# Moving the tiles that TensorE reads to other address offsets within 512 bytes

## The chip, the cores and the metric

The kernel runs on one core of a Trainium2 chip. The metric is device time in microseconds of the whole program on that core, the median of several executions. The profiled execution is one of its own, and every duration below is from it.

## The reference

One layer of a hybrid decoder on a sequence of 512 positions of width 2048, in float32:

```
h = rms_norm(x, norm1_w);  proj = h @ w_in            # 2048 -> 5648 columns
q, k, v, z, xbc, dt = split(proj)
attn = moba_attention(rms_norm(q), rms_norm(k), v)    # 8 heads x 128, blocks of 256
ssm  = grouped_rms_norm(ssd_scan(silu(conv4(xbc)), softplus(dt)) * silu(z))
x = x + concat(attn, ssm) @ w_out                     # 2048 -> 2048
h = rms_norm(x, norm2_w)
u = conv3(h @ w_up)                                   # 2048 -> 2 x 5632
x = x + (silu(u_gate) * u_val) @ w_down               # 5632 -> 2048
```

## The kernel before

Every float32 product is made of three matmuls on numbers that are cut in two: with hi the rounded part (type float32r) and lo the rest, it adds hi·hi, hi·lo and lo·hi. ScalarE makes hi (a Copy), VectorE makes lo (a subtraction).

**First stage** (to about 800 us): the input projection, attention, the scan, and the output projection. The activations lie in 16 tiles `A0` to `A15` (hi) and 16 tiles `B0` to `B15` (lo), each 128 x 512 float32, in the pool `ab`. Weights come by DMA into `raw` (three buffers), pieces of up to 528 columns are cut into `hi` and `lo` (three buffers each, pool `w`). All matmuls of this stage have the source line 183, a helper that paces them. There are two forms. In `acc<-A,hi`, `acc<-B,hi`, `acc<-A,lo` the activations are the moving operand (512 columns) and a 128 x 128 block of weights is loaded as the stationary one. In `acc<-hi,A`, `acc<-lo,A`, `acc<-hi,B` it is the other way round, and 256, 264 or 512 columns of weights move. In the names of the profile the moving operand of these stands first.

**Second stage** (from about 800 us): up-projection and down-projection, with a Strassen-like scheme of seven products in place of eight. A group is one block of rows of output (44 groups for the up-projection, 24 for the down-projection); a group has seven items, and an item is one product: eight blocks of 128 x 128 weights (seven in 16 of the down-projection's groups), each with three matmuls of 256 columns. Line 1286 is hi·hi, line 1287 hi·lo (the same weights loaded again), line 1289 lo·hi; an item is 8 x (1286, 1287) and then 8 x 1289, 24 matmuls in a row. The weights of an item lie in `hi2` (three buffers of 4096 bytes, made by ScalarE at line 1041) and `lo2` (two buffers, VectorE, line 1050). The moving operand is one of seven combinations of the activations, the kinds KT1, KT3, K11, KT2, K21, K22, KT4, held in the tiles `cmb0` to `cmb6` in this order. A kind is a tile of 16384 bytes a partition, [hi or lo][8 blocks][256 columns], so each matmul's moving operand starts at the tile's address plus a multiple of 1024 bytes, and each block of weights at its tile's address plus a multiple of 512. `cmb0` to `cmb4` lie in the pool `cmb` on the right side of the memory, `cmb5` and `cmb6` in the pool `w2` on the left side, behind the weights. The items of a group come in the order P5, P3, P1, P4, P6, P2, P7, which are the kinds KT1, K22, K11, KT4, KT2, K21, KT3 (P3 and P4 belong to the group before). P2 alone writes a tile `y`; the others write a tile `x`.

What a tile's address is, is decided by the pools: a pool lays its tiles one behind the other, in the order in which they are first asked for. The order of all instructions is written out in the program (slots, and a planner for the first stage that uses estimated costs); no address has a part in it.

Of the kernel before, what the change touches and what calls it, by code (L numbers as in the profile page):

```python
# [20 lines left out]
F32 = mybir.dt.float32  # L21
F32R = mybir.dt.float32r
# [37 lines left out]

KT1, KT3, K11, KT2, K21, K22, KT4 = range(7)
PLACE = [4, 5, 0, 6, 2, 3, 7]
KIND = {"P5": KT1, "P7": KT3, "P1": K11, "P6": KT2, "P2": K21, "P3": K22, "P4": KT4}


# [122 lines left out]
def body(ctx, tc, xT, wi, wz, wo, wu, wd0, wd1, wd2, pp, pf, outT, dbg={}):  # L188
    nc = tc.nc
    clk = {"pe": 0.0, "act": 0.0, "dve": 0.0, "pool": 0.0, "last": ("pe", 0.0)}  # L190
    V, A_, T, G = (Paced(e, k, clk) for e, k in
                   ((nc.vector, "dve"), (nc.scalar, "act"), (nc.tensor, "pe"), (nc.gpsimd, "pool")))

    consts = ctx.enter_context(tc.tile_pool(name="consts", bufs=1))
    pstack = ExitStack()
    psum = pstack.enter_context(tc.tile_pool(name="psum", bufs=4, space=bass.MemoryType.PSUM))
    dram = ctx.enter_context(tc.tile_pool(name="scratch", bufs=1, space=bass.MemoryType.DRAM))
    ab, cw, work = ExitStack(), ExitStack(), ExitStack()
    wpool = ab.enter_context(tc.tile_pool(name="w", bufs=3))
    abp = ab.enter_context(tc.tile_pool(name="ab", bufs=1))  # L200
    cpool = cw.enter_context(tc.tile_pool(name="c", bufs=1, side="right"))
    wk = work.enter_context(tc.tile_pool(name="work", bufs=1, side="right"))
# [7 lines left out]


    RW = 1024
    BEHIND = 2.5
    pieces = []

# [14 lines left out]
    def issue_dma(upto):  # L230
        while state["dma"] <= min(upto, len(raw_q) - 1):
            ci = state["dma"]
            src, width = raw_q[ci]
            r = wpool.tile([128, RW], F32, name="raw")
            if ci == 0:
                nc.sync.dma_start(r[:, :512], src[:, :512])
                nc.sync.dma_start(r[:, 512:width], src[:, 512:])
            else:
                nc.sync.dma_start(r[:, :width], src)
            raws[ci] = r  # L240
            state["dma"] += 1

    def issue_split(upto):
        while state["split"] <= min(upto, len(pieces) - 1):
            i = state["split"]
            ci, o, w, _ = pieces[i]
            issue_dma(ci)
            h = wpool.tile([128, 528], F32R, name="hi")
            l = wpool.tile([128, 528], F32R, name="lo")
            src = raws[ci][:, o:o + w]  # L250
            clk["last"] = ("pe", clk["pe"])
            A_.activation(h[:, :w], src, AF.Copy)
            V.tensor_tensor(l[:, :w], src, h[:, :w].bitcast(F32), op=OP.subtract)
            his[i] = (h, l)
            ready[i] = clk["dve"]
            state["split"] += 1

    def dump(n, ap):
        if n in dbg:
            nc.sync.dma_start(dbg[n], ap)  # L260


    A = [abp.tile([128, S], F32R, name=f"A{k}") for k in range(NK)]
    B = [abp.tile([128, S], F32R, name=f"B{k}") for k in range(NK)]
    C = [cpool.tile([128, S], F32, name=f"C{k}") for k in range(NK)]
    par = consts.tile([128, NPC], F32, name="par")
# [12 lines left out]
    def pc(name, i=0, n=1):  # L279
        o = _PC[name] + i  # L280
        return (p2["par"] if name[0] == "f" else par)[:, o:o + n]
# [54 lines left out]
    def step(e):  # L336
        clk["last"] = ("pe", clk["pe"])
        old = clk["pe"], clk["act"], clk["dve"], clk["pool"]
        e[3] = 0
        try:  # L340
            say = next(e[0])
        except StopIteration:
            if e in gens:
                gens.remove(e)
            return
        if old != (clk["pe"], clk["act"], clk["dve"], clk["pool"]):
            e[1] = max(clk[k] for k in ("pe", "act", "dve", "pool") if k != "pool" or clk[k] != old[3]) + 0.3
        if e not in gens:
            e[2] = e[2] or say == "soon"
            gens.append(e)  # L350
        elif say == "soon":
            e[2] = True
        elif say == "later":
            e[2] = False

    def advance(force=False):

        for e in list(gens):
            e[3] += 1
            ready_ = clk["pe"] >= e[1]  # L360
            if force or (e[2] and (ready_ or e[3] > 1)) or \
                    (ready_ and max(clk["act"], clk["dve"]) < clk["pe"] + BEHIND):
                step(e)
# [308 lines left out]
    def tok_use(k0, nk, cols, box, done):  # L672

        def use(h, l):
# [5 lines left out]
            for kk, t in order:  # L680
# [3 lines left out]
                o = box["acc"][t][:, :cols]  # L684
                T.matmul(o, A[k][:, ts_], h[:, cc], start=k == 0, stop=False)
                T.matmul(o, A[k][:, ts_], l[:, cc], start=False, stop=False)
                T.matmul(o, B[k][:, ts_], h[:, cc], start=False, stop=k == NK - 1)
                if k == NK - 1:
                    done(t, box["acc"][t])
        return use  # L690

    XR = lambda k: (A[k], B[k])

# [8 lines left out]
    def prep_x(k):  # L702
        t = ssq_box[k]
        A_.activation(A[k], t, AF.Copy, scale=pc("nw1", k))
        V.scalar_tensor_tensor(B[k], t, pc("nw1", k), A[k].bitcast(F32), op0=OP.mult, op1=OP.subtract)

# [131 lines left out]
    def split_mix(i):  # L838
# [5 lines left out]
        dump("mix%d" % k, C[k])  # L844
        A_.activation(A[i], C[k], AF.Copy)
        V.tensor_tensor(B[i], C[k], A[i].bitcast(F32), op=OP.subtract)

    p2 = {}

    def phase2():  # L850
        while gens:
            advance(True)
        work.close()
        cw.close()
        p2["cmb"] = ctx.enter_context(tc.tile_pool(name="cmb", bufs=1, side="right"))
        p2["kinds"] = [None] * 7
        for t in (KT1, KT3, K11, KT2, K21):
            p2["kinds"][t] = cmb_tile(t)
        p2["pool"] = work.enter_context(tc.tile_pool(name="work2", bufs=1, side="right"))
        p2["ssq"] = rbc  # L860

    def cmb_tile(t):

        pool = p2["cmb"] if t < K22 else p2["cmbl"]
        return pool.tile([128, 2, 8, 256], F32R, name="cmb%d" % t)
# [26 lines left out]
    def g_x2(acc, i):  # L892

        if "pool" not in p2:
            phase2()
            for n in range(4):
                load_xin(n)
# [17 lines left out]
        for n, ts in enumerate(((KT1, K11), (KT2, K21, KT3))):  # L915
            sums(V, g, n)
            for t in ts:
                o = p2["kinds"][t][:, :, i // 2, :]
                A_.activation(o[:, 0], g[:, PLACE[t], :], AF.Copy)
                V.tensor_tensor(o[:, 1], g[:, PLACE[t], :], o[:, 0].bitcast(F32), op=OP.subtract)  # L920
        nc.sync.dma_start(xd[:, i // 2], g[:, 3:8:4, :])
        square(t_, i)

    last_acc = []
    MR = lambda k: (A[k], B[k])
    out_start = len(pieces)
# [17 lines left out]
    V.memset(u_t[:, 0:3], 0.0)  # L944
    prep_x(0)
    issue_split(0)
    sq_x(0)
    issue_split(1)
    prep_x(1)
    sq_x(1)  # L950
    prep_x(2)
    issue_split(2)
    sq_x(2)
    mix_at = {}
# [15 lines left out]
    lp = ctx.enter_context(tc.tile_pool(name="w2", bufs=1, reuse_waits="tile"))  # L970
# [3 lines left out]
    def side_tile(pool, shape, name, bufs=1):  # L974
        return pool.tile([128] + shape, F32, name=name, bufs=bufs)
# [68 lines left out]
    def split_lo(k):  # L1044
        if k >= len(items):
            return
        n = cols(items[k][0])
        h, src = parts[k]
        l = lp.tile([128, 1024], F32R, name="lo2", bufs=2)
        ve.tensor_tensor(l[:, :n], src[:, :n], h[:, :n].bitcast(F32), op=OP.subtract)  # L1050
        parts[k] = (h, l)
# [24 lines left out]
    def b_load(k):  # L1076
# [6 lines left out]
        else:  # L1083
            ld = side_tile(box["pool"], [4, 256], "ld", box["depth"])
        sy.dma_start(ld[:, :m, :], gd[p][:, 4 * h:4 * h + m, PLACE[t], :])
        lds.append(ld)
# [34 lines left out]
    def x_load(n):  # L1121
        if n < 4:
            x_ld.append(side_tile(box["pool"], [4, 256], "ld", 3))
            sy.dma_start(x_ld[n], xd[:, 4 * (n % 2):4 * (n % 2) + 4, n // 2, :])

    def x_split(n):
        t, h = (K22, KT4)[n // 2], n % 2
        if h == 0:
            up_kinds[t] = cmb_tile(t)
        o = up_kinds[t][:, :, 4 * h:4 * h + 4, :]  # L1130
        se.activation(o[:, 0], x_ld[n], AF.Copy)
        ve.tensor_tensor(o[:, 1], x_ld[n], o[:, 0].bitcast(F32), op=OP.subtract)
        x_load(n + 3)

    for n, slot in enumerate((2, 4, 5, 6)):
        at(slot, x_split, n)
# [117 lines left out]
    def step_slot(slot):  # L1254
        run(slot)
        if slot > -2:
            split_lo(slot + 2)
        run(slot, after)
        split(slot + 3)

    for slot in range(min(events), -3):
        run(slot)
    step_slot(-3)
    split_lo(0)
    spawn(g_x2(last_acc[0], NK - 1))
    while gens:
# [5 lines left out]
    for k, (gi, x) in enumerate(items):  # L1272
# [6 lines left out]
        h, l = parts.pop(k)  # L1279
        bk = g["kinds"][KIND[x]]  # L1280
        n = g["n"]
# [36 lines left out]
```

## Time and profile before

| | us |
|---|---|
| median of 3 runs | 2114.42 (2113.61 to 2114.91) |
| the profiled execution's own time | 2114.84 |
| its span from the first to the last instruction | 2113.1 |
| TensorE matmul busy | 2073.9 (98%) |
| TensorE weight load busy | 1949.7 (92%) |
| VectorE busy | 1583.5 (75%) |
| ScalarE busy | 988.3 (47%) |

A matmul's busy time runs from its start to its end, and the next one begins long before that end. The rate of TensorE is therefore read from the distance between two starts, or from the number of matmuls in a stretch, not from the mean time of one.

### The profile page before, as it was taken

How to read it: one execution, taken by the hardware profiler on the slowest of the kernel's cores; microseconds unless marked ns; L12 is line 12 of the kernel's file. 1: busy time of each engine (PE TensorE's matmuls, PEld its weight loads, DVE VectorE, ACT ScalarE, POOL GpSimd, SP SyncE). 2: the span in 40 equal slices, each digit the busy share in tenths (PEclk: the TensorE clock that was granted, in tenths of full speed). 3: DMA queues.
4: the chain of work that ended last, by engine and by line, in shares of the span. 5: the costliest groups of instructions: out<-in, count | busy, mean ns of one | idle time of the engine just before them, and what ended most of it. 6: DMA issues, size and time to landing. Idle time of an engine off the chain costs nothing.

```text
span 2113.1 us, 37694 instructions
## 1 busy us (share of the span) xinstructions
PE 2073.9 (98%) x15366; PEld 1949.7 (92%) x15366; DVE 1583.5 (75%) x2251; ACT 988.3 (47%) x1433; POOL 207.9 (10%) x107
## 2 busy tenths in 40 slices
PE   9999999999999998999999999999999899999999
PEld 7888887888888878999999999999999899899999
DVE  6545555345555558999999999999999977977976
ACT  5433435244344435555555555555555534534532
POOL 0020000000000001111110111011111111101110
PEclk9999999999999999999999999999999999999999
DMA  5233222332225535445444444454455667856763
GB/s 194 75 115 91 71 75 76 99 101 80 80 70 172 165 129 188 158 141 189 160 156 165 170 168 155 157 183 158 142 188 201 215 215 242 274 184 231 260 201 120
DMA packets 114396, 328.18 MB, mean 155 GB/s; under 512 B 10736, under 2 KB 35120, under 8 KB 111408
## 3 DMA queue, kind: packets, MB, share of 16 engines
q1 hardware_dynamic: 114224, 325.78, 45.5%
q8 instruction: 120, 1.97, 0.4%
q14 instruction: 52, 0.43, 0.1%
HBM read 283.77 MB, written 41.98 MB: 154 GB/s over the span
## 4 chain that ended last, share of the span: by engine, by line
PE 88%; DVE 7%; issue 2%; ACT 1%; DMA 1%; SPq 0%; DVEq 0%; POOL 0%; ACTq 0%; POOLq 0%
PE acc L183 29%; PE x L1289 16%; PE x L1286 16%; PE x L1287 16%; PE sm L183 4%; PE y L1289 3%; PE y L1287 3%; PE y L1286 3%; DVE lo L1050 2%; DVE cmb L1097 1%; DVE lo L183 1%; DVE acc L1151 0%; DVE s L1024 0%; DMA raw<-wi 0%; DVE s L1030 0%
## 5 line engine op out<-in xcount | busy, mean ns | idle before, releaser
L1287 PE MATMUL x<-cmb,hi 128*128 128x256 f32 x3168 | 755.0, 279 | 12.5 <-DVE cmb L1097 10.9
L1286 PE MATMUL x<-cmb,hi 128*128 128x256 f32 x3168 | 755.8, 279 | 11.5 <-ACT cP L1166 5.4
L1287 PEld LDWEIGHTS x<-cmb,hi 128*128 128x128 f32 x3168 | 599.3, 189 | 15.2 <-DVE cmb L1097 13.4
L1286 PEld LDWEIGHTS x<-cmb,hi 128*128 128x128 f32 x3168 | 598.7, 189 | 13.4 <-issue 7.5
L1289 PE MATMUL x<-cmb,lo 128*128 128x256 f32 x3168 | 434.3, 279 | 2.6 <-DVE lo L1050 2.6
L1289 PEld LDWEIGHTS x<-cmb,lo 128*128 128x128 f32 x3168 | 397.2, 189 | 3.6 <-DVE lo L1050 3.4
L183 DVE TENSOR_TENSOR lo<-raw,hi 128x512 fp32r<-128x512 f32 (+1 forms) x240 | 164.4, 691 | 243.0 <-ACT hi L183 228.5
L1041 ACT ACTIVATE hi<-s 128x1024 fp32r<-128x1024 f32 (+1 forms) x201 | 201.0, 1000 | 287.3 <-DVE s L1024 192.2
L1017 POOL TENSOR_TENSOR rawb<-rawa,rawb 128x1024 f32<-128x1024 f32 (+1 forms) x68 | 169.7, 2496 | 1308.1 <-DVE s L1024 1070.8
L183 PE MATMUL acc<-A,hi 128*128 128x512 f32 x704 | 281.5, 400 | 0.5 <-ACT hi L183 0.5
L183 PE MATMUL acc<-A,lo 128*128 128x512 f32 x704 | 277.9, 395 | 0.1
L183 PE MATMUL acc<-B,hi 128*128 128x512 f32 x704 | 276.8, 393 | 0.0
L183 ACT ACTIVATE hi<-raw 128x512 fp32r<-128x512 f32 (+1 forms) x240 | 149.6, 629 | 256.2 <-PE acc L183 220.3
L1050 DVE TENSOR_TENSOR lo<-s,hi 128x1024 fp32r<-128x1024 f32 (+1 forms) x201 | 238.6, 1187 | 18.8 <-issue 18.8
L1050 DVE TENSOR_TENSOR lo<-rawa,hi 128x1024 fp32r<-128x1024 f32 (+1 forms) x204 | 242.0, 1186 | 3.6 <-PE x L1289 3.6
L1041 ACT ACTIVATE hi<-rawa 128x1024 fp32r<-128x1024 f32 (+1 forms) x204 | 209.5, 1028 | 40.0 <-PE x L1287 39.9
L183 PEld LDWEIGHTS acc<-A,lo 128*128 128x128 f32 x704 | 132.1, 188 | 33.0 <-DVE lo L183 2.1
L183 PEld LDWEIGHTS acc<-A,hi 128*128 128x128 f32 x704 | 132.7, 188 | 29.5 <-ACT hi L183 1.8
L183 PEld LDWEIGHTS acc<-B,hi 128*128 128x128 f32 x704 | 132.5, 188 | 28.3
L1166 ACT ACTIVATE cP<-x 128x256 f32<-128x256 f32 x132 | 50.9, 385 | 214.0 <-PE x L1289 214.0
L183 PE MATMUL acc<-hi,A 128*128 128x256 f32 (+2 forms) x448 | 135.4, 302 | 0.7 <-DVE u L183 0.7
L183 PE MATMUL acc<-lo,A 128*128 128x256 f32 (+2 forms) x448 | 133.5, 298 | 0.0
(204 smaller groups left out, 2777.2 us busy)
## 6 DMA issues: line engine op xcount, KB each, us to landing
rawa<-wu SPq DMA_DIRECT2D x176, 512.0 KB, 3.6
raw<-wi SPq DMA_DIRECT2D x79, 512.0 KB, 3.6
rawa<-wd SPq DMA_DIRECT2D x64, 448.0 KB, 4.1
rawb<-wu SPq DMA_DIRECT2D x44, 512.0 KB, 4.5
gd<-gt SPq DMA_DIRECT2D x22, 1024.0 KB, 4.6
raw<-wo SPq DMA_DIRECT2D x32, 512.0 KB, 3.6
rawa<-wd SPq DMA_DIRECT2D x32, 512.0 KB, 4.4
ld<-gd SPq DMA_DIRECT2D x27, 512.0 KB, 6.4
```

The lines of the kernel that those rows point to most:

```text
L183: return fn(out, *args, **kw)
L1017: po.tensor_tensor(r, raw[gi, "11"][:, :n], r, op=OP.subtract)
L1041: se.activation(h[:, :n], src[:, :n], AF.Copy)
L1050: ve.tensor_tensor(l[:, :n], src[:, :n], h[:, :n].bitcast(F32), op=OP.subtract)
L1097: ve.tensor_tensor(lo, ld[:, :m, :], hi.bitcast(F32), op=OP.subtract)
L1166: se.activation(g[x], X[:, 256:] if x == "P5" else X[:, :256], AF.Copy)
L1286: pe.matmul(out, w, bk[:, 0, q, :], start=fresh and q == 0, stop=False, skip_group_check=True)
L1287: pe.matmul(out, w, bk[:, 1, q, :], start=False, stop=False, skip_group_check=True)
L1289: pe.matmul(out, l[:, q * 128:(q + 1) * 128], bk[:, 0, q, :], start=False, stop=q == n - 1, skip_group_check=True)
```

## The change

Tiles that nothing reads or writes (`space`) are asked for between the others, so that the tiles behind them move; the scratch that the program reserves for dynamic DMAs at the bottom of the memory is cut from 16384 to 1024 bytes to make room; and `hi` and `lo` of the first stage are 640 columns wide in place of 528. No transfer of this kernel uses that scratch: all are issued on SyncE's queue with fixed addresses.

Addresses within a partition, modulo 512 bytes:

| tile | before | after |
|---|---|---|
| first stage: `A`, moving or stationary | 32 | 256 |
| first stage: `B` | 32 | 384 |
| first stage: `hi`, three buffers | 160, 224, 288 | 0, 0, 0 |
| first stage: `lo`, three buffers | 352, 416, 480 | 0, 0, 0 |
| second stage: `hi2`, three buffers | 32 | 32 |
| second stage: `lo2`, two buffers | 32 | 0 |
| KT1 (`cmb0`, P5) | 480 | 224 |
| K22 (`cmb5`, P3) | 32 | 32 |
| K11 (`cmb2`, P1) | 480 | 288 |
| KT4 (`cmb6`, P4) | 32 | 352 |
| KT2 (`cmb3`, P6) | 480 | 0 |
| K21 (`cmb4`, P2) | 480 | 480 |
| KT3 (`cmb1`, P7) | 480 | 96 |

No engine gets another instruction or another order. TensorE, GpSimd and SyncE have the same waits as before. Where the pools of the second stage take over the addresses of the first stage's, two waits shift: at the first group's hi2 and acc_s, ScalarE and VectorE wait for other matmuls of the first stage than before, since other `A` and `B` tiles lay there.

```
+GAPS = {KT1: 384, KT3: 192, K11: 224, KT2: 480}
...
+    def space(pool, n):
+        pool.tile([128, n // 4], F32, name="space%d" % next(spaces), bufs=1)
...
+    WT = 640
...
-            h = wpool.tile([128, 528], F32R, name="hi")
-            l = wpool.tile([128, 528], F32R, name="lo")
+            h = wpool.tile([128, WT], F32R, name="hi")
+            l = wpool.tile([128, WT], F32R, name="lo")
...
+    space(wpool, 352)
+    space(abp, 256)
     A = [abp.tile([128, S], F32R, name=f"A{k}") for k in range(NK)]
+    space(abp, 128)
     B = [abp.tile([128, S], F32R, name=f"B{k}") for k in range(NK)]
...
         for t in (KT1, KT3, K11, KT2, K21):
             p2["kinds"][t] = cmb_tile(t)
+            if t in GAPS:
+                space(p2["cmb"], GAPS[t])
...
+        if k == 0:
+            space(lp, 480)
         l = lp.tile([128, 1024], F32R, name="lo2", bufs=2)
...
         t, h = (K22, KT4)[n // 2], n % 2
+        if n == 0:
+            space(lp, 32)
+        if n == 2:
+            space(lp, 320)
...
-    nc = _bacc.Bacc("TRN2", target_bir_lowering=False, num_devices=1)
+    nc = _bacc.Bacc("TRN2", target_bir_lowering=False, num_devices=1, dynamic_dma_scratch_size=1024)
```

## Rows read from the trace of the kernel before

**Rows 1.** The page: busy time of the engines, then slices of the span for TensorE, VectorE and TensorE's granted clock.

```profile
PE 2073.9 (98%) x15366; PEld 1949.7 (92%) x15366; DVE 1583.5 (75%) x2251; ACT 988.3 (47%) x1433; POOL 207.9 (10%) x107
...
PE   9999999999999998999999999999999899999999
...
DVE  6545555345555558999999999999999977977976
...
PEclk9999999999999999999999999999999999999999
```

**Rows 2.** The page: shares of the chain of work that ended last, by engine.

```profile
PE 88%; DVE 7%; issue 2%; ACT 1%; DMA 1%; SPq 0%; DVEq 0%; POOL 0%; ACTq 0%; POOLq 0%
```

**Rows 3.** Who waited for whom, TensorE from 800 us to the end: total us, times, longest.

```profile
PE x L1287 <- DVE cmb L1097: 10.9, 11, 2.3
PE x L1286 <- ACT cP L1166: 5.4, 2, 5.0
```

**Rows 4.** Busy time by stretch (us, busy and instructions of each engine, granted clock, DMA share, GB/s): first stage with 256 moving columns, first stage with 512, one group of the up-projection, 200 us of it, 200 us of the down-projection.

```profile
474.42:491.33 16.91, 16.91 (x146) 16.91 (x145) 9.64 (x22) 7.25 (x16) 0.40 (x1) 1.00 0.23 64
700.00:780.00 80.00, 80.00 (x346) 64.69 (x345) 41.76 (x76) 32.31 (x63) 0.00 (x0) 1.00 0.42 137
1245.61:1264.97 19.36, 19.36 (x170) 19.36 (x169) 18.01 (x24) 10.07 (x13) 2.46 (x1) 1.00 0.40 138
1000.00:1200.00 200.00, 200.00 (x1738) 200.00 (x1737) 186.28 (x232) 103.21 (x134) 24.61 (x10) 1.00 0.45 161
1800.00:2000.00 200.00, 192.73 (x1646) 190.43 (x1645) 167.51 (x199) 94.28 (x97) 29.28 (x11) 1.00 0.69 237
```

**Rows 5.** Busy time by stretch, TensorE alone, three items that follow each other: KT1 (P5), K22 (P3), K11 (P1). Each stretch runs from the item's first matmul to the next item's first (24 matmuls; 26 counted, two reach over an edge).

```profile
1262.25:1264.97 2.72, 2.72 (x26) 1.00 0.96 378
1264.97:1267.83 2.86, 2.86 (x26) 1.00 0.84 345
1267.83:1270.57 2.74, 2.74 (x26) 1.00 0.64 239
```

**Rows 6.** Timeline of TensorE (start, duration): the end of that KT1 item, the K22 item, the start of the K11 item. A row with x8 is the eight matmuls of line 1289, from the first start to the last end.

```profile
1263.73 0.28 PE L1287 MATMUL x<-cmb,hi 128*128 128x256 f32 x1
1263.84 0.28 PE L1286 MATMUL x<-cmb,hi 128*128 128x256 f32 x1
1263.95 0.28 PE L1287 MATMUL x<-cmb,hi 128*128 128x256 f32 x1
1264.07 1.07 PE L1289 MATMUL x<-cmb,lo 128*128 128x256 f32 x8
...
1266.39 0.28 PE L1286 MATMUL x<-cmb,hi 128*128 128x256 f32 x1
1266.51 0.28 PE L1287 MATMUL x<-cmb,hi 128*128 128x256 f32 x1
1266.63 0.28 PE L1286 MATMUL x<-cmb,hi 128*128 128x256 f32 x1
1266.75 0.28 PE L1287 MATMUL x<-cmb,hi 128*128 128x256 f32 x1
1266.87 1.12 PE L1289 MATMUL x<-cmb,lo 128*128 128x256 f32 x8
```

**Rows 7.** Timeline of TensorE, two items of the kind K21 (P2, tile y): the first group's, which begins behind other work, and one of a later group.

```profile
809.78 0.28 PE L1287 MATMUL y<-cmb,hi 128*128 128x256 f32 x1
...
811.43 0.28 PE L1287 MATMUL y<-cmb,hi 128*128 128x256 f32 x1
811.54 1.11 PE L1289 MATMUL y<-cmb,lo 128*128 128x256 f32 x8
...
1276.29 0.28 PE L1287 MATMUL y<-cmb,hi 128*128 128x256 f32 x1
...
1277.87 0.28 PE L1287 MATMUL y<-cmb,hi 128*128 128x256 f32 x1
1277.99 1.07 PE L1289 MATMUL y<-cmb,lo 128*128 128x256 f32 x8
```

**Rows 8.** Groups of instructions of TensorE up to 800 us, shapes apart: busy us, mean ns of one, idle before.

```profile
L183 PE MATMUL acc<-A,hi 128*128 128x512 f32 x704 | 281.5, 400 | 0.5 <-ACT hi L183 0.5
L183 PE MATMUL acc<-A,lo 128*128 128x512 f32 x704 | 277.9, 395 | 0.1
L183 PE MATMUL acc<-B,hi 128*128 128x512 f32 x704 | 276.8, 393 | 0.0
L183 PE MATMUL acc<-hi,A 128*128 128x256 f32 x256 | 73.5, 287 | 0.0
...
L183 PE MATMUL acc<-hi,A 128*128 128x264 f32 x128 | 36.8, 287 | 0.7 <-DVE u L183 0.7
...
L183 PE MATMUL acc<-hi,A 128*128 128x512 f32 x64 | 25.1, 392 | 0.0
```

**Rows 9.** Timeline of TensorE in the first stage: 512 moving columns.

```profile
553.39 0.39 PE L183 MATMUL acc<-A,hi 128*128 128x512 f32 x1
553.61 0.39 PE L183 MATMUL acc<-B,hi 128*128 128x512 f32 x1
553.84 0.39 PE L183 MATMUL acc<-A,lo 128*128 128x512 f32 x1
554.07 0.39 PE L183 MATMUL acc<-A,hi 128*128 128x512 f32 x1
```

**Rows 10.** Timeline of ScalarE where the second stage begins, with the idle time before and its releaser.

```profile
799.63 1.06 ACT L1041 ACTIVATE hi<-acc_s 128x1024 fp32r<-128x1024 f32 x1 [0.95 <-DVE acc_s L1028]
```

More of the change, by code (lines that the diff above doesn't have):

```diff
@@ L192, in body @@
                    ((nc.vector, "dve"), (nc.scalar, "act"), (nc.tensor, "pe"), (nc.gpsimd, "pool")))
+    spaces = iter(range(100))
     consts = ctx.enter_context(tc.tile_pool(name="consts", bufs=1))
```

## The prediction

> **What bounds the kernel now.** I read the busy shares first, then the chain of waits, then who waits for whom, then stretches with their counts, and last the timeline. TensorE is busy for 98% of the span and its granted clock stands at 9 or more in all 40 slices, the higher of its two levels, 2.4 GHz [rows 1]; the chain that ended last is 88% TensorE [rows 2]. From 800 us on its longest wait in total for another engine is 10.9 us, for VectorE's cutting of the down-projection's operands at line 1097 [rows 3]. So time can be won almost only by letting TensorE start its matmuls closer together.
>
> How close they stand is read from stretches. One group of the up-projection, 168 matmuls, takes 19.36 us (170 counted, two reach over an edge) [rows 4]. Item by item it isn't even: KT1 takes 2.72 us for 24 matmuls, 0.1133 each; K22, which follows, 2.86; K11 after it 2.74 [rows 5]. The timeline shows the same work in each: in the K22 item the starts settle at steps of 0.12, and its eight last matmuls take 1.12 from first start to last end against 1.07 for KT1 [rows 6]. Nothing waits in any of the three, the clock is 1.00 in all, and DMA is busiest (0.96) in the fastest of them [rows 5]. What differs is where the moving operand lies: KT1 and K11 at 480 modulo 512, K22 at 32, the offset of its weights too. KT4 is the other kind at 32.
>
> The offset is not all of it. K21 at 480 runs at (1277.99 - 1276.29) / 15 = 0.1133 in a later group, but at (811.54 - 809.78) / 15 = 0.1173 in the first, where it begins behind other work, and keeps that pace to its end [rows 7]. So one pair of offsets can hold TensorE in two rhythms, and which one it falls into hangs on how it comes in. That is the main reason why I can't name each item's pace after the change.
>
> **The change part by part.** No instruction is added, removed or reordered; only addresses move. The sum is made against the profiled execution (span 2113.1, own time 2114.84), whose time is 0.4 us above the median 2114.42; I take differences and set them against the median.
>
> *The two slow kinds.* With seven items at 2.72 a group would take 19.04 instead of 19.36: 0.32 us, of which 2 x 0.14 are the slow items and 2 x 0.02 the items behind them, which first have to get back into step [rows 4, 5]. There are 44 groups in the up-projection, and the down-projection's 24 have 176 blocks of rows for seven products, as many as 22 full groups: 66 x 0.32 = 21 us. KT4 leaves the offset of its weights; K22 stays at 32 with hi2 at 32, and only its lo·hi third gets another partner (lo2 at 0). I still take the whole 21, since a kind's rhythm is also set by the item ahead, which changes for every item. If K22 stays as it is for its hi2 part, two thirds of one kind's share, about 7 us, are lost.
>
> *The changes of offset within and between items.* Before, three of a group's seven borders between items (KT2, K21, KT3, KT1) change no offset at all. After it, every item brings a new moving offset, and inside each item the weights go from 32 (hi2) to 0 (lo2). The nearest row for such a change that ends in the fast rhythm is the 2.74 item: 0.02 [rows 5]. Ends: nothing, and 0.02 twice an item, 66 x 7 x 0.04 = 18 us. I take about a quarter, +5 us: 0.02 is the price of leaving the slowest rhythm, and a change from one fast pair to another may cost less.
>
> *The first stage.* 512 moving columns: 3 x 704 + 3 x 64 = 2304 matmuls [rows 8], at 80 / 344 = 0.2326 in a stretch that holds nothing else [rows 4]. The tightest run of starts is (554.07 - 553.39) / 3 = 0.2267, twice 0.1133 [rows 9]. If all ran so: 2304 x 0.0059 = -14 us. If all went at twice 0.12: 2304 x 0.0074 = +17 us. Now every one of these matmuls meets another pair of offsets, A at 256, B at 384, weights always at 0; before, the weights went round six offsets. A fixed pattern can lock well or badly. I take a third of the gain, -5 us. 256 and 264 moving columns: 768 + 384 matmuls [rows 8] at 16.91 / 144 = 0.1174 [rows 4]; ends -1152 x 0.0041 = -5 and +1152 x 0.0026 = +3; I take 0.
>
> *What costs nothing.* VectorE is busy 18.01 of 19.36 us a group [rows 4]; against 19.04 that is 95%, so it still follows, and what its cover is worth shows only below 18.1 us a group. In the down-projection TensorE already has 200 - 192.73 = 7.3 us of idle time in 200 [rows 4]; a faster TensorE may turn some of the 7 us won there (22 x 0.32) into waiting, which the range covers. The two waits that shift at the start of the second stage: ScalarE's first split there waited 0.95 us for VectorE's sum, not for TensorE [rows 10]; an earlier release behind it frees nothing. The smaller scratch is used by no transfer.
>
> Sum: -21 + 5 - 5 + 0 = -21 us, 2114.4 - 21 = 2093.
>
> **A rule that speaks against it.** The rows show one and the same item 5% longer by where its moving operand lies [rows 5]. The Trainium skill, "SBUF — State Buffer", section "Who interferes with whom", says that TensorE has two independent read ports, one for the moving operand and one for the weight load, and that it never waits on anyone. By that no address could matter, the sum would be nothing and the time 2114; the trace disagrees, unless something other than the offset tells the two slow kinds apart, which is the second case below.
>
> **The rivals.** First (my forecast): most items settle in the fast rhythm or near it, 2093; the terms' better ends, -21 - 14 - 5 = -40, and the worse, without K22's 7 and with the full 18 for the changes, -21 + 7 + 18 = +4, give 2074 to 2118 as its outer bounds, the middle of it 2080 to 2108. For it speaks that five of seven kinds keep 0.1133 for whole items with one pair of offsets [rows 5, 7].
>
> Second: no change, 2114. The two slow kinds are also the only two that lie in the left pool, beside their weights; if it is that neighbourhood, not the offset modulo 512, that slows them, they stay slow, for they stay there. Against it: K21 in the right pool was slow too, in the first group [rows 7]. For it: the two kinds are slow in every group, whatever came before.
>
> Third: slower, by a mechanism of its own: with another offset at every border and within every item, TensorE falls into the middle rhythm of 0.1173 and stays in it, as K21 did in the first group. Seven items of 24 x 0.1173 = 2.815 make 19.71 a group, +0.35, x 66 = +23 us: 2137; with the first stage at its bad end 2154. It decides from the third slow kind on: each kind kept at 2.86 costs 66 x 0.14 = 9 us, and two are slow now. For it: the first stage, where offsets change from matmul to matmul, has a mean of 0.1174 for 256 columns, that very pace [rows 4].
>
> Fourth: better than any row of an item. If an even start lets a matmul go below 0.1133, down to the 0.22 / 2 = 0.11 of one single step in the first stage, 553.39 to 553.61 [rows 9], 66 x 168 x 0.0033 = 37 us more: 2056. VectorE then has 18.0 of some 18.5 us and begins to hold it up. Against it: 0.1133 is exact over whole items, as a floor is. The Trainium skill, "TensorE: Matmul & The Clock Gate", section "Wait — 56ns, not 53.3ns?", gives columns / 2.4 GHz plus about 2.5 ns, by which 256 columns would need 109.2 ns, an estimate; no item here comes that low.
>
> **How the numbers follow.** Forecast case 0.58, no change 0.12, slower 0.20, below the floor 0.10. About 0.2%, 4 us, is what a measurement of this kernel can tell from no change. The forecast case gives 0.04 of its share to "within 0.2%" with its worst corner, the second case the rest: faster 0.64, same 0.16, slower 0.20. The range goes from 2072, the better end of the forecast case, to 2130, which takes in the second case and about half of the third; outside lie most of the fourth (0.08) and half of the third (0.10).
>
> **What would show it.** Right: items of 2.72 to 2.74 us for KT4 and for most others, groups of 19.0 to 19.15 us, and the first stage's 512-column stretch at or under 0.232. The terms are told apart by item: K22 at 2.86 again says that the offset to hi2 alone decides; an item whose last eight matmuls go at another pace than its first sixteen says that the pair with lo2 counts by itself. Wrong: groups over 19.4 us with the steps at 0.117 or 0.12 (third case), or KT4 unchanged at 2.86 although its offset moved (second).

## The result: 27 us slower

The changed kernel takes 2141.3 us (median of 4, 2140.64 to 2141.97), the kernel before 2114.66 (median of 4, 2113.61 to 2116.89). The ratio is 1.0125 with a 95% interval of 1.0107 to 1.0142: slower by 1.25%, on the other side of no change from the forecast of 2093 and above the range's upper end of 2130.

The page of the changed kernel, busy time and granted clock, against [rows 1]:

```profile
PE 2107.3 (98%) x15366; PEld 1984.8 (93%) x15366; DVE 1585.2 (74%) x2251; ACT 987.8 (46%) x1433; POOL 208.1 (10%) x107
...
PEclk9999999999999999999999999999999999999999
```

The same 15366 matmuls make TensorE busy for 33.4 us more. The mean granted clock of the two profiled executions is 0.998 before and 0.995 after, which is not the reason: the changed kernel takes 2140.64 us at 0.995 and 2140.81 at 0.998. Who waited for whom, TensorE from 800 us on, against [rows 3]:

```profile
PE x L1305 <- DVE cmb L1111: 9.4, 11, 1.7
PE x L1304 <- ACT cP L1184: 5.5, 2, 5.0
```

So neither wait grew by more than 0.1 us, and the engines beside TensorE do the same work in nearly the same time. What changed is how close the matmuls start. Busy time by stretch, all engines, columns as in [rows 4] and the same kinds of stretch:

```profile
474.42:491.33 16.91, 16.91 (x145) 16.91 (x144) 8.97 (x21) 7.22 (x15) 0.98 (x1) 1.00 0.20 64
700.00:780.00 80.00, 80.00 (x348) 65.02 (x347) 41.77 (x77) 32.42 (x63) 0.00 (x0) 1.00 0.43 139
1272.87:1292.70 19.83, 19.83 (x171) 19.83 (x169) 18.15 (x24) 10.06 (x15) 2.46 (x1) 1.00 0.51 186
1000.00:1200.00 200.00, 200.00 (x1696) 200.00 (x1696) 182.88 (x229) 101.25 (x132) 24.64 (x10) 1.00 0.44 161
1800.00:2000.00 200.00, 196.32 (x1650) 195.02 (x1650) 161.67 (x192) 91.36 (x93) 26.99 (x10) 1.00 0.67 232
```

The first stage is as before: 145 for 146 matmuls, 348 for 346. In the second stage a group takes 19.83 us for 19.36, and 200 us hold 1696 matmuls for 1738. Two starts in each kernel say where the 27 us fall: the first matmul of the second stage and the first of the down-projection, in the kernel before:

```profile
791.31 0.36 PE L1286 MATMUL x<-cmb,hi 128*128 128x256 f32 x1 [1.98 <-issue]
...
1649.45 0.28 PE L1286 MATMUL x<-cmb,hi 128*128 128x256 f32 x1
```

and the same two after the change:

```profile
791.66 0.46 PE L1304 MATMUL x<-cmb,hi 128*128 128x256 f32 x1 [1.97 <-issue]
...
1669.53 0.28 PE L1304 MATMUL x<-cmb,hi 128*128 128x256 f32 x1
```

The first stage costs 0.35 us, the up-projection 20.08 - 0.35 = 19.7 (44 groups x 0.47 would be 20.7), and the rest of the span's 27.1, some 7 us, falls behind 1669 us. There 22 x 0.47 = 10.3 would have been expected; in the 200 us shown, idle time of TensorE shrank from 7.3 us to 200 - 196.32 = 3.7, so part of the slower pace probably went into time in which TensorE had waited before.

The seven items of that group, TensorE alone, in the order KT1, K22, K11, KT4, KT2, K21, KT3, against [rows 5]:

```profile
1272.87:1275.69 2.82, 2.82 (x26) 1.00 0.83 320
1275.69:1278.53 2.84, 2.84 (x26) 1.00 0.85 348
1278.53:1281.39 2.86, 2.86 (x27) 1.00 0.60 209
1281.39:1284.23 2.84, 2.84 (x26) 1.00 0.57 190
1284.23:1287.06 2.83, 2.83 (x26) 1.00 0.00 0
1287.06:1289.85 2.79, 2.79 (x26) 1.00 0.00 0
1289.85:1292.70 2.85, 2.85 (x27) 1.00 0.72 233
```

Not one item has the 2.72 that KT1 had. DMA says nothing about it: the two items without a byte moved take 2.83 and 2.79. The timeline of the K21 item, whose offset with hi2 (480 with 32) is the old one, shows how even that one loses time:

```profile
1287.07 0.28 PE L1304 MATMUL y<-cmb,hi 128*128 128x256 f32 x1
...
1287.31 0.28 PE L1304 MATMUL y<-cmb,hi 128*128 128x256 f32 x1
...
1287.77 0.28 PE L1304 MATMUL y<-cmb,hi 128*128 128x256 f32 x1
...
1288.79 0.28 PE L1305 MATMUL y<-cmb,hi 128*128 128x256 f32 x1
1288.91 1.11 PE L1307 MATMUL y<-cmb,lo 128*128 128x256 f32 x8
```

It comes in slowly (0.24 for two steps), has the fast step of 0.1133 from 1287.77 to 1288.79 (9 steps in 1.02), and goes slow again with the eight matmuls on lo2: 1.11 from first start to last end, (1.11 - 0.28) / 7 = 0.1186 a step, where [rows 7] have 1.07, or 0.113, in a later group. Only the partner changed there: lo2 lies at 0, not at 32.

### The profile page after: what moved, and what is told of

Its sections match the earlier page's. It is cut to its first block, busy times and chain, and to the rows that moved or that the text cites. A ratio compares the mean times of both kernels' runs of the same rounds, so it can differ in the third digit from the quotient of the medians.

```text
span 2140.2 us, 37693 instructions
## 1 busy us (share of the span) xinstructions
PE 2107.3 (98%) x15366; PEld 1984.8 (93%) x15366; DVE 1585.2 (74%) x2251; ACT 987.8 (46%) x1433; POOL 208.1 (10%) x107
## 4 chain that ended last, share of the span: by engine, by line
PE 89%; DVE 6%; DMA 2%; issue 1%; ACT 1%; SPq 0%; DVEq 0%; POOL 0%; ACTq 0%; POOLq 0%
PE acc L184 29%; PE x L1307 16%; PE x L1304 16%; PE x L1305 16%; PE sm L184 4%; PE y L1307 3%; PE y L1304 3%; PE y L1305 3%; DVE lo L1064 1%; DVE cmb L1111 1%; DMA rawa<-wd 1%; DMA ld<-gd 1%; DMA t<-xT 1%; DVE lo L184 0%; DVE s L1036 0%
## 5 line engine op out<-in xcount | busy, mean ns | idle before, releaser
L1304 PE MATMUL x<-cmb,hi 128*128 128x256 f32 x3168 | 773.7, 282 | 9.7 <-ACT cP L1184 5.5
L1305 PE MATMUL x<-cmb,hi 128*128 128x256 f32 x3168 | 773.7, 282 | 9.4 <-DVE cmb L1111 9.4
L1307 PE MATMUL x<-cmb,lo 128*128 128x256 f32 x3168 | 443.4, 282 | 1.8 <-DVE lo L1064 1.8
L1307 PEld LDWEIGHTS x<-cmb,lo 128*128 128x128 f32 x3168 | 405.4, 189 | 2.0 <-DVE lo L1064 2.0
```

Of the source, the lines that this page charges most:

```text
L1304: pe.matmul(out, w, bk[:, 0, q, :], start=fresh and q == 0, stop=False, skip_group_check=True)
L1305: pe.matmul(out, w, bk[:, 1, q, :], start=False, stop=False, skip_group_check=True)
L1307: pe.matmul(out, l[:, q * 128:(q + 1) * 128], bk[:, 0, q, :], start=False, stop=q == n - 1, skip_group_check=True)
```

## The experiments

Three theories stood against each other. R (P in the first expectations, which leave out the rhythms): the pair's own difference of offsets (moving operand less weights) sets which rhythms an item can have. B: it is the change of offset, at borders and inside items, that costs, whatever the offsets. N: it is the place in the left pool, beside the weights, that slows K22 and KT4. Times are medians with the lowest and highest; each ratio is to the kernel before on the same chip. The edits of e1, e5 and e8 are to the kernel before; those of e2, e3, e4, e6 and e7 are to the changed kernel, whose first stage they keep; e9's is shown against e2.

**e1_all480: the kernel before, with K22 and KT4 at 480 like the rest.** It is the forecast's first term by itself.

```
         t, h = (K22, KT4)[n // 2], n % 2
+        if n == 0:
+            lp.tile([128, 448 // 4], F32, name="space_k", bufs=1)
```

> The kernel before with one change: K22 and KT4 moved within the left pool so that they too start at 480 modulo 512; all weights stay at 32. Theory P (the pair of offsets of moving operand and weights sets the pace, and 480 with 32 is a fast pair): all seven items 2.72 us, groups 19.04, 66 x 0.32 = 21 us less, 2093. Theory B (changes of offset between and within items break the rhythm; a common offset keeps it): no border left, also 2093. Theory N (K22 and KT4 are slow because they lie in the left pool beside the weights): nothing changes, 2114.

Four executions: 2095.24, 2128.85, 2134.98 and 2135.40 us, at granted clocks of 0.994 to 0.998, against 2114.46 for the kernel before at the same clocks. Only the first was profiled; 200 us of it, TensorE alone:

```profile
1000.00:1200.00 200.00, 200.00 (x1767) 1.00 0.46 166
```

1767 against 1738: 200 / 1766 = 0.1133, every item at the fast step, so K22 and KT4, in their old pool, run as fast as the others once they lie at 480. N falls. And the forecast's -21 us is nearly reached (2114 - 21 = 2093). But that was one execution of four; the other three were 14 to 21 us slower than before. They left no trace, so why is not shown; a slow rhythm kept through much of the second stage, as in e2, would explain it. The profiled execution itself began in the slow rhythm: its K11 item of the first group still has sixteen starts from 822.08 to 823.85, 0.118 a step. Then VectorE's lo2 became ready late, at 822.65 + 1.22 = 823.87, only 0.1 us before the first matmul on it:

```profile
822.65 1.22 DVE L1050 TENSOR_TENSOR lo<-rawa,hi 128x1024 fp32r<-128x1024 f32 x1
...
823.97 1.13 PE L1291 MATMUL x<-cmb,lo 128*128 128x256 f32 x8
...
826.75 1.07 PE L1291 MATMUL x<-cmb,lo 128*128 128x256 f32 x8
```

The eight matmuls on it take 1.13, and the next item's 1.07, the fast rhythm, which then holds to where the down-projection begins. In e2 the lo2 of the same item is ready 0.8 us ahead, and the slow rhythm stays. That this one hold-up chose the rhythm is argued from one execution.

**e2_all224: all seven kinds at 224, hi2 and lo2 both at 32, the rest of the change kept.** No change of offset is left in the second stage.

```
-GAPS = {KT1: 384, KT3: 192, K11: 224, KT2: 480}
+GAPS = {K21: 256}
...
-        if k == 0:
-            space(lp, 480)
...
         if n == 0:
-            space(lp, 32)
-        if n == 2:
-            space(lp, 320)
+            space(lp, 192)
```

> The changed kernel with all seven kinds at the same offset, 224, and hi2 and lo2 both at 32: no border between or within items, but another pair. Theory P: every item at the pace that KT1 shows at 224 with 32 in the changed kernel, 0.1175 a matmul, 19.74 us a group, 2114 + 66 x 0.38 = 2139. Theory B: no borders, so the fast rhythm, 19.04 us a group, 2093.

2129.77 us (2127.78 to 2131.61), ratio 1.0070 [1.0054, 1.0087]. One execution has both rhythms. TensorE alone: 200 us and one 24-matmul item of the up-projection, then an item of 21 matmuls of the down-projection:

```profile
1000.00:1200.00 200.00, 200.00 (x1701) 1.00 0.45 161
1262.13:1264.96 2.83, 2.83 (x26) 1.00 0.00 0
1750.02:1752.40 2.38, 2.38 (x24) 1.00 0.96 324
```

2.83 / 24 = 0.118 and 2.38 / 21 = 0.1133, with the same tiles at the same offsets. The slow rhythm holds from the first group's K21 item (809 us) almost to the end of the up-projection; the fast one comes only where the down-projection begins, among waits of TensorE such as this:

```profile
1675.01 0.39 PE L1301 MATMUL x<-cmb,hi 128*128 128x256 f32 x1 [1.51 <-DVE cmb L1109]
```

So B falls as the main cause: with no change of offset at all, the up-projection is slow. A difference of 192 has two rhythms, and kept the one it had fallen into across items and groups.

**e3_after_lo32: the change with lo2 back at 32.** The kinds' offsets alone (with the first stage's).

```
-        if k == 0:
-            space(lp, 480)
...
-        if n == 0:
-            space(lp, 32)
```

> The changed kernel with lo2 back at 32; the seven offsets of the kinds as changed. Theory P: only K21's last eight matmuls get the fast pair back, 66 x 8 x 0.005 = 3 us, the other kinds keep 0.1175 to 0.12, 2138 to 2140. Theory B: half of the borders (those inside items) are gone, so about half of the loss of 27 us, near 2128.

2137.03 us (2135.56 to 2138.14), 1.0106 [1.0091, 1.0121], +23 us. One group, TensorE alone, in the order KT1 (224), K22 (32), K11 (288), KT4 (352), KT2 (0), K21 (480), KT3 (96), all with weights at 32:

```profile
1271.41:1274.13 2.72, 2.72 (x26) 1.00 0.89 345
1274.13:1277.00 2.87, 2.87 (x27) 1.00 0.78 321
1277.00:1279.88 2.88, 2.88 (x27) 1.00 0.67 228
1279.88:1282.71 2.83, 2.83 (x27) 1.00 0.57 191
1282.71:1285.54 2.83, 2.83 (x26) 1.00 0.00 0
1285.54:1288.30 2.76, 2.76 (x27) 1.00 0.00 0
1288.30:1291.12 2.82, 2.82 (x26) 1.00 0.60 221
```

Here each kind's own pair shows, since hi2 and lo2 agree. Only the two kinds at 224 and 480 are fast (K21's 2.76 has slow first steps). K11 at 288 is as slow as K22 at 32 (2.88 / 24 = 0.120), and 288 is 32 + 256: what counts repeats after 256 bytes, not 512. KT3 and KT4, 96 and 352, are again a pair 256 apart, at 2.82 and 2.83. KT2 at 0 takes 2.83. That these paces are not only taken over from the item ahead shows in KT3, which follows an item that ends in the fast rhythm, (1.07 - 0.28) / 7 = 0.113:

```profile
1287.39 1.07 PE L1303 MATMUL y<-cmb,lo 128*128 128x256 f32 x8
```

KT1 takes 2.72 here and 2.82 in the changed kernel, with the same pair with hi2. There its sixteen matmuls on hi2 are slow too, (1274.63 - 1272.87) / 15 = 0.1173, behind KT3's last eight, which meet lo2 at a difference of 96 there and of 64 here:

```profile
1272.87 0.28 PE L1304 MATMUL x<-cmb,hi 128*128 128x256 f32 x1
...
1274.63 0.28 PE L1305 MATMUL x<-cmb,hi 128*128 128x256 f32 x1
```

**e4_first: the change's first stage, the second stage's offsets as before.**

```
-GAPS = {KT1: 384, KT3: 192, K11: 224, KT2: 480}
+GAPS = {}
...
-        if k == 0:
-            space(lp, 480)
...
-        if n == 0:
-            space(lp, 32)
-        if n == 2:
-            space(lp, 320)
```

> The changed kernel's first stage (hi, lo at 0, A at 256, B at 384, small scratch) with the offsets of before in the second stage. Both theories: the stretches with 512 moving columns stand at 0.232 a matmul before and after, so the first-stage part is worth nothing and the time is 2113 to 2116. If the first stage had lost or won, the time would leave that band by the same amount.

2114.61 us (10 executions, 2113.87 to 2116.07), 0.9999 [0.9990, 1.0009]. The first stage's new offsets, the smaller scratch and the wider hi and lo tiles are together worth nothing that this can tell.

**e5_reset1: the kernel before, with KT4 alone at 480.** K22 stays at its slow difference of 0, once a group.

```
         t, h = (K22, KT4)[n // 2], n % 2
+        if n == 2:
+            lp.tile([128, 448 // 4], F32, name="space_k2", bufs=1)
```

> The kernel before with KT4 alone moved to 480; K22 stays at 32, the offset of the weights. Theory R (at 480 and 224 with 32 there are two rhythms, 0.1133 and 0.1177, and one is kept from item to item until something breaks it; an item whose operands lie at the same offset runs at 0.12 and hands over to the fast rhythm, so it sets all behind it right): K22 at 2.86 in each group, everything else 2.72, 66 x 0.16 = 11 us less than before, 2104, and the same in every execution. Theory L (the rhythm is luck, K22 has no part in it): either 2095 or up to 2135 from one execution to the next, as with all kinds at 480.

2104.33 us (2103.37 to 2105.66), 0.9955 [0.9940, 0.9970], half of the 21 us, and in each of four executions. In each group one slow item goes, one stays, and behind the one that stays the fast rhythm is found again. The first group shows it: the last eight matmuls of KT1, in the slow rhythm, of K22, and of K11:

```profile
818.67 1.10 PE L1291 MATMUL x<-cmb,lo 128*128 128x256 f32 x8
...
821.52 1.12 PE L1291 MATMUL x<-cmb,lo 128*128 128x256 f32 x8
...
824.31 1.07 PE L1291 MATMUL x<-cmb,lo 128*128 128x256 f32 x8
```

TensorE has no idle time between them.

**e6_alt: KT1, KT3, KT2 at 224, K11, K21, KT4 at 480, K22 at 32, weights at 32.** Offsets change at nearly every border, but all fast kinds have the difference 192 modulo 256.

```
-GAPS = {KT1: 384, KT3: 192, K11: 224, KT2: 480}
+GAPS = {KT2: 256, K11: 256, KT3: 256}
...
-        if k == 0:
-            space(lp, 480)
...
-        if n == 0:
-            space(lp, 32)
         if n == 2:
-            space(lp, 320)
+            space(lp, 448)
```

> The changed kernel with KT1, KT3, KT2 at 224, K11, K21, KT4 at 480, K22 at 32 and hi2, lo2 at 32: a new moving offset at six of seven borders, but only pairs that are alike modulo 256. Theory R with a period of 256 bytes: 224 and 480 are the same pair, the rhythm passes over the borders, K22 sets it right, 2104. Theory B (each change of offset costs): the borders between 224 and 480 break the fast rhythm, 2120 or more.

2105.41 us (2104.37 to 2106.96), 0.9960 [0.9946, 0.9975], as e5. Five items that follow each other, KT1 (224), K22 (32), K11 (480), KT4 (480), KT2 (224):

```profile
1279.13:1281.85 2.72, 2.72 (x27) 1.00 0.92 352
1281.85:1284.71 2.86, 2.86 (x26) 1.00 0.10 36
1284.71:1287.45 2.74, 2.74 (x27) 1.00 0.59 191
1287.45:1290.17 2.72, 2.72 (x27) 1.00 0.56 193
1290.17:1292.89 2.72, 2.72 (x27) 1.00 0.00 0
```

The border from 480 to 224 costs nothing (2.72 behind 2.72), so B falls here too, and 224 serves as well as 480.

**e7_shift32: the pattern of the kernel before, with every tile of the second stage 32 bytes further.** Five kinds at 0, K22, KT4, hi2 and lo2 at 64, so that all are multiples of 64.

```
-GAPS = {KT1: 384, KT3: 192, K11: 224, KT2: 480}
+GAPS = {K21: 480}
...
+        if k == 0:
+            space(lp, 32)
         h = lp.tile([128, 1024], F32R, name="hi2", bufs=3)
...
-        if k == 0:
-            space(lp, 480)
...
-        if n == 0:
-            space(lp, 32)
-        if n == 2:
-            space(lp, 320)
```

> All offsets of the second stage of before moved on by 32: five kinds at 0, K22, KT4, hi2 and lo2 at 64; every difference as before, but all at multiples of 64. Theory R by differences: items of 2.72, 2.86 and 2.74 as before, 2114. If the place against multiples of 64 counts by itself, all items change pace alike: at 0.1094 or below 2050 to 2080, or the slow rhythm throughout, 2130 or more.

2113.27 us (10 executions, 2112.67 to 2115.92), 0.9999 [0.9989, 1.0008]. No item went near the 0.1094 of the expectation. A shift of both operands by 32 bytes has no weight; moving the kinds alone (e1) or lo2 alone (e8) has.

**e8_lo0: the kernel before, with only lo2 moved from 32 to 0.**

```
+        if k == 0:
+            lp.tile([128, 480 // 4], F32, name="space_lo", bufs=1)
         l = lp.tile([128, 1024], F32R, name="lo2", bufs=2)
...
+        if n == 0:
+            lp.tile([128, 32 // 4], F32, name="space_k0", bufs=1)
```

> The kernel before with only lo2 moved, from 32 to 0; all kinds and hi2 as before. Theory P (the pair alone): the last eight matmuls of the five kinds at 480 go at about 0.1185 as K21's do in the changed kernel, those of the two slow kinds at 0.117, the first sixteen as before: 66 x (5 x 8 x 0.0052 - 2 x 8 x 0.003) = 11 us more, 2125. Theory R: the fast rhythm doesn't outlive the eight matmuls with lo2, so hi parts behind them fall to 0.1177 too, another 66 x 5 x 16 x 0.0044 = 23 us at most, 2125 to 2148.

2125.32 us (2122.20 to 2126.50), 1.0052 [1.0037, 1.0067], +11 us. Timeline of TensorE, the KT3 item:

```profile
1261.56 0.28 PE L1290 MATMUL x<-cmb,hi 128*128 128x256 f32 x1
...
1263.26 0.28 PE L1291 MATMUL x<-cmb,hi 128*128 128x256 f32 x1
1263.37 1.11 PE L1293 MATMUL x<-cmb,lo 128*128 128x256 f32 x8
```

Sixteen starts at (1263.26 - 1261.56) / 15 = 0.1133, then eight at (1.11 - 0.28) / 7 = 0.1186: the pair of 480 with 0 is slow by itself. The next item, back at 480 with 32, is fast at once (sixteen starts at 0.1133), so the second theory of the expectation, that the fast rhythm does not outlive these eight, falls.

**e9_all160: all kinds at 160, hi2 and lo2 at 32, a difference of 128.** As e2, with other sizes of the spaces.

```
-GAPS = {K21: 256}
+GAPS = {K21: 320}
...
-            space(lp, 192)
+            space(lp, 128)
```

> The changed kernel with all seven kinds at 160 and hi2, lo2 at 32: a difference of 128, not seen yet in a steady run. With 0 (or 256): 0.12; 64 (or 320): 0.1177; 192 (or 448): 0.1133 or 0.1177. If the pace falls in even steps with the difference modulo 256, 128 gives a single rhythm between the neighbours, 0.115 to 0.1177: 2114 + 66 x (168 x 0.1165 - 19.36) = 2128, within 2110 to 2140. If 128 holds the fast rhythm alone, 2093 and the same in every execution.

2147.91 us (2147.46 to 2149.74), 1.0160 [1.0143, 1.0177], the slowest of all. 200 us, TensorE alone:

```profile
1000.00:1200.00 200.00, 200.00 (x1688) 1.00 0.45 160
```

200 / 1687 = 0.1186 a step.

**e10_first192 and e11_first0: e5 with the first stage at one difference**, 192 where activations move and so 64 where weights do (`A`, `B` at 32, hi, lo at 96), and 0 (all at 32). The edit of e10 against e5; in e11 the first space is 32 and the last line is left out:

```
-            h = wpool.tile([128, 528], F32R, name="hi")
-            l = wpool.tile([128, 528], F32R, name="lo")
+            if i == 0:
+                space(wpool, 96)
+            h = wpool.tile([128, WT], F32R, name="hi")
+            l = wpool.tile([128, WT], F32R, name="lo")
...
+    space(wpool, 352)
+    space(abp, 448)
```

> The second stage as in the run with one kind left at 32 (2104), and in the first stage A and B at 32 with all buffers of hi and lo at 96: where activations move (2112 matmuls of 512 columns) the difference is 192 modulo 256 in every one. Theory R carried over to 512 columns: they may lock at 0.2267 in place of 0.2320, 2112 x 0.0055 = 12 us less, 2092. If 512 columns don't lock, or lock in their slow rhythm: 2104 or up to 2114.

> As the run before, but hi and lo of the first stage at 32, the offset of A and B: difference 0 in all matmuls of the first stage. Theory R carried over: the slowest pair, twice 0.12 for 512 columns, 2304 x 0.0075 = 17 us more, and 0.12 for 256 columns, 768 x 0.002 = 2 us more: 2104 + 19 = 2123. If offsets don't matter in the first stage: 2104.

e10: 2107.51 us (2106.25 to 2108.43), 0.9967 [0.9954, 0.9980], 3 us more than e5. e11: 2098.38 us (2097.31 to 2099.41), 0.9924 [0.9909, 0.9939], 6 us less than e5. The stretch of 512 moving columns, first e10:

```profile
700.00:780.00 80.00, 80.00 (x344) 1.00 0.43 138
```

and e11:

```profile
700.00:780.00 80.00, 80.00 (x355) 1.00 0.44 144
```

The sign is the other way round from the second stage: with 512 columns the difference 0 is the good one, 80 / 353 = 0.2266, and 192 gives 80 / 342 = 0.234. Both expectations, carried over from 256 columns, missed. The 256-column matmuls of e11 go at 0.12, the pace of K22:

```profile
479.81 0.28 PE L184 MATMUL acc<-hi,B 128*128 128x256 f32 x1
...
480.05 0.28 PE L184 MATMUL acc<-lo,A 128*128 128x256 f32 x1
```

2304 x 0.0060 = 14 us won at most and 1152 x 0.0026 = 3 lost would leave 11; 6 were measured, and the second stage begins 6.5 us earlier than in e5 (784.71 for 791.24). Where the rest went wasn't traced. e11 beats both kernels, by 16 us the one before and by 43 the changed one.

## Why the prediction was wrong

**The bound was right.** TensorE's spacing decides: the same instructions took from 2098 to 2148 us (medians) by addresses alone, and no wait of TensorE for another engine grew by more than 0.1 us.

**The step that failed is "I still take the whole 21, since a kind's rhythm is also set by the item ahead".** It took two kinds off their pace of 0.12 and left the other five at 0.1133, though the change moved four of them (all but K21); for that it paid only the borders' +5. The rows held a reason not to: the five were fast with one pair, 480 with 32, and the only other pair known, 32 with 32, was slow. After the change only K21 keeps the known fast pair with hi2, KT1 gets an equal one (224), and the other five have the differences 0 (K22, K11), 64 (KT4, KT3) and 224 (KT2), all slow in e3. So six of seven items went at 2.82 to 2.86 and K21 at 2.79, 19.83 us a group, where the sum had 19.04. The neighbour does matter, but it didn't make a slow pair fast: a slow item at difference 0 hands the fast rhythm on to a pair that has it (e5, e6), while KT1 went slow, probably by KT3's eight matmuls at 96 ahead of it (e3). The 21 us themselves were well sized: e1's profiled execution won 19, one of four.

**The term for changes of offset, +5 (0 to 18), was priced as a border cost and is none.** Between equal differences a border is free (e6). What costs inside the items is the pair with lo2 at 0, by itself +11 us (e8), as the prediction's own test had it: last eight matmuls at another pace than the first sixteen. The parts don't add: kinds +23 (e3), lo2 +11 (e8), both +27, since an item that is slow already has less to lose on lo2 (K22's last eight even win, 0.117 for 0.120).

**The first stage, -5 (-14 to +17), was 0** (e4): two patterns of differences with nearly the same mean step (346 and 348 matmuls counted in 80 us). Of the end of -14, difference 0 for all pairs gave 6 (e11); 192 cost 3 (e10). The forecast case's outer bound of 2118 left out this term's own bad end, +17, and the +3 of 256 columns: with them it would have been 2138.

**What was priced at nothing cost nothing that e4 can tell:** scratch, wider tiles; and TensorE's waits did not grow.

**The rivals.** The third named the outcome, 2137 for 2141, and the pace, 19.71 us a group for 19.83; it had a chance of 0.20. Its mechanism, a middle rhythm kept because offsets change at every border, is not what happened in the main: e2 is slow without any change, e6 fast with many, and K22, K11, KT4, KT3 and KT2 are each slow by their own pair. Only KT1 fits it, a pair that can be fast held at 0.1173. That its number came so near is mostly luck. The second, the left pool, fell with e1. The fourth stayed out of sight: no stretch went below 0.1133. By the Trainium skill, "TensorE: Matmul & The Clock Gate", section "Wait — 56ns, not 53.3ns?", 256 columns would need 109.2 ns, an estimate; the fastest execution here, e1's, has 113.3 over 200 us.

## What to carry to other kernels

Where one engine issues the same instruction back to back and its steps differ by a few per cent without a wait, compare the addresses of its operands: here the differences of moving operand and weights modulo 256 bytes moved the whole time by over 2% (2098 to 2148 us). A pace read for one pair of addresses holds for that pair; give a new pair no price before it has been seen, not the best one of the trace. And time a rhythm that can be lost in several executions: the fastest execution of all (e1, 2095 us) had three others of the same kernel at 2129 to 2135, while one slow item a group that brings the rhythm back gave 2103 to 2106 in all four (e5).

## What the runs showed of the hardware

Steps of TensorE for 128x256 float32r matmuls with a new weight block each, by (moving offset - weight offset) modulo 256 bytes, at granted clock 1.00:

| difference | us a step | from |
|---|---|---|
| 0 | 0.120 once settled | K11 in e3, K22 [rows 6] |
| 64 | 0.118 | KT3, KT4 in e3 |
| 128 | 0.1186 | e9 |
| 192 | 0.1133 or 0.118, kept until TensorE is held up or another pair passes | e1, e2, e5, e6 |
| 224 | 0.118 to 0.1186 | KT2 in e3, lo2 part in e8 |

With 512 columns the order is another: 0.2266 at difference 0 (e11), 0.234 at 192 (e10). Differences of 32 and 96 occurred only in the last eight matmuls of items (lo2 at 0): the K22 item of the changed kernel has 0.117 there, the KT3 item 0.120. A difference of 160 was not tried.

The Trainium skill, "SBUF — State Buffer", section "Who interferes with whom", says that TensorE reads its two operands by independent ports and never waits on anyone. The runs disagree as far as addresses go: how the two operands of this one engine lie to each other makes a matmul's step 4 to 6% longer or not. Whether it is the reads that collide, no run shows. Why the distance between them counts modulo 256, and why it does so differently at 256 and 512 columns, stays open, and so does what decides which rhythm a pair at 192 falls into: in e1 and e2 it changed where TensorE was held up, but not which hold-up leads to which.
